# A two-layer decoder trunk: sinks loaded once, loads and stores on other queues, the combination in two parts, C's keys in two homes

## The chip, the cores and the metric

One core of a Trainium2 chip runs the whole program. The core has five engines that each work through a list of instructions of their own, in order: TensorE (PE in the rows; its weight loads PEld), VectorE (DVE), ScalarE (ACT), GpSimd (POOL) and SyncE (SP). A DMA is started by an instruction in the list of SyncE or of GpSimd, so it has a place in that list too: what stands behind a DMA that must wait for its buffer waits as well. The metric is the device time of one execution in microseconds (us), and a kernel's time is the median of its runs.

## The reference

The program computes two decoder layers on an input x of 512 rows by 1024 columns, in float32. One projection of x gives queries, keys, values and gates for three kinds of attention, A, B and C; their outputs are gated, projected and added, and a convolutional gated feed-forward part follows. The part that matters here, cut to its core:

```python
def hybrid_mixer(x, ...):
    proj = x @ w_in
    # A: 3 head groups (window, dilation), 8 heads each; the groups' outputs are
    #    weighted by a softmax over their log denominators
    for gi, (window, dil) in enumerate(A_GROUPS):
        o_g, lse_g = dilated_group_attention(...)
    wts = softmax(stack(lses), axis=0);  o_a = einsum('gbsh,gbshd->bshd', wts, stack(outs))
    # B: sliding window of 128, 8 heads, a learned sink logit per head in max and denominator
    m = maximum(logits.max(-1), sink);  p = exp(logits - m);  denom = p.sum(-1) + exp(sink - m)
    # C: latent attention, 8 heads, causal, 64 columns of key without and 32 with rotary position
    logits = (q_nope . k_nope + q_rope . k_rope) * scale
    merged = sum(sigmoid(gate_i) * (o_i @ w_branch[i]) for i in 3)
    return merged @ w_out
```

## The kernel before, in words

**Arithmetic.** float32 operands are split into a high part (ScalarE copies it) and a low part (VectorE subtracts), by `split_to` (L184, L185), and for weights at L76 and L77. A product is then three TensorE instructions, `mm3` (L178 to L180). Most are 128x128 weights against 512 columns; at the full clock such a one starts 0.227 us after the last.

**Stages of a layer.** The latents of C (`latp`), then A's projections with A's attention running between them, then B's projections, then a series of steps: gates (`gp`, 24 instructions each) and branch projections (`bp`, 12 each), in the order that the table `STEPS` gives, and then the output projection and the feed-forward part. The branch projections take A's output first, then B's, then C's. Attention runs in the gaps of the projections: `Attention.gap` adds time to a budget and `step` takes items from a queue. An item has three phases, a step apart: `scores` (scp, the exponentials), `turn` (normalisation and the transposes `ptp`) and `values` (`op`, the output). Its `cost` is what it takes from the budget. So where a gap falls, items of A, B and C stand between gate and branch instructions. A scheduler then fixes the order on each engine; the lists of instructions shown below are its result.

**Buffers.** 23 slots of the pool `sp` (4 KB in each of 128 partitions) are handed round between weights' successors, queries, keys, probabilities, loaded outputs (`od`) and their split forms (`oth`, `otl`), and rotary intermediates (`rq`, `rh`, `rl`). A new tile waits until the last use of the one whose slot it takes, and a DMA out of a slot counts as a use until it has landed.

**The places that the change touches.**

- *Sinks.* In each layer a tile `sink` of 128x2x8 is loaded on SyncE (L394, called at L424) and negated on VectorE (L425). There is one buffer, so layer 1's load waits until B of layer 0 has used the last sink.
- *Outputs through DRAM.* Each attention's output `ot` is stored by GpSimd into `o_dram` (L562 for B, L1001 for A, L810 for C). `load_oT` (L471) loads it as two tiles `od` on SyncE, before the branch projections. `split_oT` transposes A's (`otp`, L485) and splits all.
- *A's combination.* Rows of A's groups are stored by GpSimd to `arow` (L639); `Combine` loads them (`ct`, L973, on SyncE) in its `turn` and weighs them on VectorE (`cmx` at L988 and on) in its `values`, for two halves of the heads with four tiles each.
- *C.* `RopeC.run` rotates queries, splits them into `rh` and `rl`, stores these to `rope_q` with GpSimd (L892) and copies the keys' rotary half into `ckh` and `ckl` (L897). There is one such pair of key tiles. `PairC.run` loads the queries' rotary part (`cqh`, `cql`, L945, GpSimd) and writes the pair's keys into `ckh` and `ckl`, for each of four pairs of heads; four tiles of queries follow it (`ItemC`), tile t with t+1 key tiles. The values of tiles 0 and 1, and of 2 and 3, are one run of `op` (8 and 16 instructions), whose result takes two ScalarE copies (L808), two VectorE additions (L809) and two stores (L810).

## Time and profile before

| | us |
|---|---|
| median of 3 runs | 2081.39 |
| lowest, highest | 2080.52, 2083.09 |
| the profiled execution | 2081.52 |
| its span | 2079.8 |

The span is what the trace covers; 1.7 us of the profiled execution lie around it. [...] A row of a timeline gives the start in us from the span's start, the duration, the engine and line, the operation as out<-in, and in brackets how long the engine had been idle before it and what ended that. Where several equal instructions follow each other they share a row, with xN. Matmul rows overlap, since TensorE is pipelined: the time from start to start is what one costs.

### The profile page before, as it was taken

How to read it: one execution, taken by the hardware profiler on the slowest of the kernel's cores; microseconds unless marked ns; L12 is line 12 of the kernel's file. 1: busy time of each engine (PE TensorE's matmuls, PEld its weight loads, DVE VectorE, ACT ScalarE, POOL GpSimd, SP SyncE). 2: the span in 40 equal slices, each digit the busy share in tenths (PEclk: the TensorE clock that was granted, in tenths of full speed). 3: DMA queues.
4: the chain of work that ended last, by engine and by line, in shares of the span. 5: the costliest groups of instructions: out<-in, count | busy, mean ns of one | idle time of the engine just before them, and what ended most of it. 6: DMA issues, size and time to landing. Idle time of an engine off the chain costs nothing. (4 is left out here: it accounts for less than half of the span.)

```text
span 2079.8 us, 28299 instructions
## 1 busy us (share of the span) xinstructions
PE 2029.4 (98%) x10466; PEld 1717.3 (83%) x10466; DVE 1235.6 (59%) x2531; ACT 906.9 (44%) x1850; POOL 204.0 (10%) x354
## 2 busy tenths in 40 slices
PE   8999999989999999999999999999999999999997
PEld 7888888878878888888888888887888888888885
DVE  5545667757646664356465546686675566635645
ACT  4544465645432343244235444655564315423431
POOL 1111211201100100000020212112110010000001
PEclk9999999989999999999999999999999999999998
DMA  6633444435336233333433333444433443333331
GB/s 183 210 88 100 129 96 130 132 75 115 101 94 193 71 92 97 98 99 97 121 104 92 93 94 118 115 132 118 117 86 95 146 118 101 97 94 103 92 96 56
DMA packets 317447, 228.13 MB, mean 110 GB/s; under 512 B 46603, under 2 KB 289244, under 8 KB 316797
## 3 DMA queue, kind: packets, MB, share of 16 engines
q1 hardware_dynamic: 306972, 204.60, 34.6%
q0 software_dynamic: 10336, 21.72, 3.7%
q8 instruction: 83, 1.36, 0.3%
q14 instruction: 56, 0.45, 0.1%
HBM read 206.63 MB, written 24.88 MB: 111 GB/s over the span
## 5 line engine op out<-in xcount | busy, mean ns | idle before, releaser
L77 DVE TENSOR_TENSOR wlo<-wraw,whi 128x1024 fp32r<-128x1024 f32 (+2 forms) x316 | 380.0, 1204 | 371.9 <-ACT whi L76 368.0
L76 ACT ACTIVATE whi<-wraw 128x1024 fp32r<-128x1024 f32 (+2 forms) x316 | 328.7, 1043 | 373.9 <-PE dnp L179 120.0
L179 PE MATMUL up<-xl,whi 128*128 128x512 f32 (+1 forms) x768 | 285.3, 372 | 0.4
L178 PE MATMUL up<-xh,whi 128*128 128x512 f32 (+1 forms) x768 | 284.2, 372 | 0.7 <-ACT xh L350 0.5
L180 PE MATMUL up<-xh,wlo 128*128 128x512 f32 (+1 forms) x768 | 284.5, 371 | 0.0
L178 PE MATMUL qkp<-xh,whi 128*128 128x512 f32 x464 | 185.2, 399 | 0.0
L180 PE MATMUL qkp<-xh,wlo 128*128 128x512 f32 x464 | 184.1, 397 | 0.0
L179 PE MATMUL qkp<-xl,whi 128*128 128x512 f32 x464 | 183.6, 396 | 0.0
L179 PEld LDWEIGHTS up<-xl,whi 128*128 128x128 f32 x768 | 144.6, 188 | 26.0 <-DVE xl L355 1.2
L178 PEld LDWEIGHTS up<-xh,whi 128*128 128x128 f32 x768 | 144.0, 188 | 26.6 <-ACT xh L350 1.6
L180 PEld LDWEIGHTS up<-xh,wlo 128*128 128x128 f32 x768 | 144.5, 188 | 25.0
L178 PE MATMUL gp<-xh,whi 128*128 128x512 f32 x384 | 153.7, 400 | 0.0
L179 PE MATMUL gp<-xl,whi 128*128 128x512 f32 x384 | 153.2, 399 | 0.0
L180 PE MATMUL gp<-xh,wlo 128*128 128x512 f32 x384 | 152.6, 397 | 0.0
L528 ACT ACTIVATE sb<-sb,row 128x128 f32<-128x128 f32 (+1 forms) x192 | 80.7, 422 | 136.3 <-DVE row L525 128.8
L179 PE MATMUL dnp<-wlo,hT 128*128 128x512 f32 x352 | 136.9, 389 | 0.0
L180 PE MATMUL dnp<-whi,hT 128*128 128x512 f32 x352 | 136.8, 389 | 0.0
L178 PE MATMUL dnp<-whi,hT 128*128 128x512 f32 x352 | 135.6, 389 | 0.0
L525 DVE CUSTOM_DVE_ANT_0 sb<-scp,bias 128x128 f32<-128x128 f32 (+1 forms) x192 | 54.5, 322 | 105.9 <-DMA arow<-row 92.2
L180 PEld LDWEIGHTS qkp<-xh,wlo 128*128 128x128 f32 x464 | 87.4, 188 | 16.8 <-issue 0.4
L178 PEld LDWEIGHTS qkp<-xh,whi 128*128 128x128 f32 x464 | 87.4, 188 | 15.8 <-ACT vv L184 0.4
L179 PEld LDWEIGHTS qkp<-xl,whi 128*128 128x128 f32 x464 | 87.5, 189 | 15.4 <-issue 0.6
(331 smaller groups left out, 4249.0 us busy)
## 6 DMA issues: line engine op xcount, KB each, us to landing
wraw<-in_w_in_dram SPq DMA_DIRECT2D x124, 512.0 KB, 3.9
wraw<-in_w_ffn_up_dram SPq DMA_DIRECT2D x88, 512.0 KB, 4.0
wraw<-in_w_ffn_down_dram SPq DMA_DIRECT2D x40, 512.0 KB, 3.8
wraw<-in_w_branch_dram SPq DMA_DIRECT2D x16, 512.0 KB, 3.7
wraw<-in_w_out_dram SPq DMA_DIRECT2D x16, 512.0 KB
arow<-row POOLq DMA_DIRECT2D x96, 66.0 KB, 2.5
ct<-arow SPq DMA_DIRECT2D x16, 396.0 KB, 3.6
od<-o_dram SPq DMA_DIRECT2D x12, 512.0 KB, 4.8
```

The lines of the kernel that those rows point to most:

```text
L76: nc.scalar.activation(hi[:, :n], raw[:, :n], AF.Copy)
L77: nc.vector.tensor_tensor(lo[:, :n], raw[:, :n], hi[:, :n].bitcast(F32), ALU.subtract)
L178: nc.tensor.matmul(o, lh, rh, start=start, stop=False)
L179: nc.tensor.matmul(o, lh, rl, start=False, stop=False)
L180: nc.tensor.matmul(o, ll, rh, start=False, stop=stop)
L525: nc.vector.tensor_tensor_reduce(v[:, h, :], pp[h], j.bias(h, nk), -j.scale, j.floor(h), ALU.add, ALU.min, self.st[:, h:h + 1])
L528: nc.scalar.activation(v[:, h, :], v[:, h, :], AF.Exp, bias=self.st[:, h:h + 1], scale=-1.0, accum_out=self.st[:, 2 + h:3 + h])
```

## The change

Four edits, in one diff:

1. One tile `sinks` holds both layers' sinks. It is loaded (two DMAs) and negated (one instruction) in layer 0 after the latents; the loads and negations of each layer are gone.
2. The loads of `od` (12) and of `ct` (16) move from SyncE's list to GpSimd's; the 8 stores to `rope_q` move from GpSimd's to SyncE's.
3. `Combine` keeps the load (cost 0.1); a new class `Weigh` has the arithmetic (cost 0.5). They stand in the queue as load 0, load 1, weigh 0, load 2, weigh 1, load 3, weigh 2, weigh 3.
4. C has two pairs of key tiles, used in turn by the pairs of heads, so the copies of the rotary half are done twice (eight instead of four on GpSimd per layer). The last tile of pairs 0 to 2 moves behind the projection of the next pair.

```diff
+    sinks = cp.tile([P, DEPTH, 2, 8], F32, name="sinks")
...
-        sink = cp.tile([P, 2, 8], F32, name="sink", tag="sink")
-        bcast(I["sinks"], l * 8, 8, sink[:, 0])
-        nc.vector.tensor_scalar(sink[:, 1], sink[:, 0], -1.0, None, op0=ALU.mult)
+        sink = sinks[:, l]
...
+        if l == 0:
+            for i in range(DEPTH):
+                bcast(I["sinks"], i * 8, 8, sinks[:, i, 0])
+            nc.vector.tensor_scalar(sinks[:, :, 1], sinks[:, :, 0], -1.0, None, op0=ALU.mult)
...
-                nc.sync.dma_start(od[a], dap(o_dram[i], a * 2 * P * 512, [[512, P], [P * 512, 2], [1, 512]]))
+                nc.gpsimd.dma_start(od[a], dap(o_dram[i], a * 2 * P * 512, [[512, P], [P * 512, 2], [1, 512]]))
...
-                att.queue.extend(Combine(hf, t) for t in range(NT))
+                cs = [Combine(hf, t) for t in range(NT)]
+                att.queue.extend((*cs[:2], Weigh(cs[0]), cs[2], Weigh(cs[1]), cs[3], Weigh(cs[2]), Weigh(cs[3])))
...
-                return self.q[0][:, h, qs], self.q[1][:, h, qs], keys_c[0][:, h, ks], keys_c[1][:, h, ks]
+                return self.q[0][:, h, qs], self.q[1][:, h, qs], self.k[0][:, h, ks], self.k[1][:, h, ks]
...
-                        nc.gpsimd.dma_start(dap(rope_q, (i * 8 + x) * 32 * S, [[64 * S, 4], [S, 32], [1, S]]),
+                        nc.sync.dma_start(dap(rope_q, (i * 8 + x) * 32 * S, [[64 * S, 4], [S, 32], [1, S]]),
                                             hl[i][:, x].bitcast(F32))
-                keys_c.extend(slot(nm, F32R).rearrange("p (h n) -> p h n", h=2) for nm in ("ckh", "ckl"))
-                for h, b in enumerate((slice(64, P), slice(0, 64))):
-                    for i in range(2):
-                        nc.gpsimd.tensor_copy(keys_c[i][b, h, :], latT[3][b, i, :])
+                for c in range(2):
+                    keys_c.append([slot(nm, F32R).rearrange("p (h n) -> p h n", h=2) for nm in ("ckh", "ckl")])
+                    for h, b in enumerate((slice(64, P), slice(0, 64))):
+                        for i in range(2):
+                            nc.gpsimd.tensor_copy(keys_c[c][i][b, h, :], latT[3][b, i, :])
...
-                nc.sync.dma_start(self.ct, dap(arow[self.hf], self.t * P * 264, [[264, P], [S * 264, 3], [1, 264]]))
+                nc.gpsimd.dma_start(self.ct, dap(arow[self.hf], self.t * P * 264, [[264, P], [S * 264, 3], [1, 264]]))
...
+        late = [i for i in items_c if isinstance(i, ItemC) and i.t == NT - 1 and i.job.c < 3]
+        for item in late:
+            items_c.remove(item)
+            items_c.insert(1 + next(n for n, i in enumerate(items_c)
+                                    if isinstance(i, PairC) and i.job.c == item.job.c + 1), item)
```

TensorE's instructions are the same in number and kind; their order differs between A's first projections and the output projection of each layer.

**VectorE where A's output is transposed, layer 0, before.** The tile sb is B's probabilities, bst their statistics, otl the low part of A's transposed output.

```order
L751 TENSOR_SCALAR sb<-sb,bst 128x256 x2
L748 RECIPROCAL bst<-bst 128x2
L185 TENSOR_TENSOR otl<-otp,oth 128x2x128 x2
L425 TENSOR_SCALAR sink<-sink 128x8
L751 TENSOR_SCALAR sb<-sb,bst 128x256 x2
L185 TENSOR_TENSOR otl<-otp,oth 128x2x128 x5
```

**The same place after.** L756 and L753 are the lines L751 and L748 of before.

```order
L753 RECIPROCAL bst<-bst 128x2 x2
L756 TENSOR_SCALAR sb<-sb,bst 128x256 x3
L185 TENSOR_TENSOR otl<-otp,oth 128x2x128
L756 TENSOR_SCALAR sb<-sb,bst 128x256
L185 TENSOR_TENSOR otl<-otp,oth 128x2x128 x6
```

The negation of the next layer's sinks is gone from between the otl splits; the rest keeps its kind and nearly its order.

**SyncE from the branch weights of A to C's second chunk, layer 0, before.** These are loads of weights (wraw, craw), of A's output and of a table.

```order
L63 DMA wraw<-in_w_branch_dram 128x4x256 x4
L471 DMA od<-o_dram_435 128x2x512 x2
L63 DMA wraw<-in_w_in_dram 128x8x128
L877 DMA ropeT<-rope_T 128x2x512
L908 DMA craw<-in_w_ukv_dram 128x4x64
L63 DMA wraw<-in_w_in_dram 128x8x128 x2
L394 DMA sink<-in_sinks_dram 128x8
L63 DMA wraw<-in_w_branch_dram 64x4x256 x2
```

**The same place after.**

```order
L63 DMA wraw<-in_w_branch_dram 128x4x256 x4
L63 DMA wraw<-in_w_in_dram 128x8x128
L886 DMA ropeT<-rope_T 128x2x512
L918 DMA craw<-in_w_ukv_dram 128x4x64
L901 DMA rope_q<-rh 4x32x512 x2
L63 DMA wraw<-in_w_in_dram 128x8x128
L901 DMA rope_q<-rl 4x32x512 x2
L63 DMA wraw<-in_w_in_dram 128x8x128
L63 DMA wraw<-in_w_branch_dram 64x4x256 x2
```

The two od loads and the sink load have left this list, and the four stores of rotated queries stand in it, around a weight load.

**TensorE at the end of C in layer 1, before.** The rows are the last gate before C's last values (op) and the branch projection of B (bp) that goes on beside them; the eight ptp of the last tile stand 17 rows ahead of the first.

```order
L178 MATMUL gp<-xh,whi 128x512
L179 MATMUL gp<-xl,whi 128x512
L180 MATMUL gp<-xh,wlo 128x512
L804 MATMUL op<-ph,cv 128x256
L178 MATMUL gp<-xh,whi 128x512
L804 MATMUL op<-ph,cv 128x128
L179 MATMUL gp<-xl,whi 128x512
L180 MATMUL gp<-xh,wlo 128x512
L178 MATMUL bp<-oth,whi 128x512
L179 MATMUL bp<-otl,whi 128x512
L804 MATMUL op<-pl,cv 128x128
L804 MATMUL op<-ph,cv 128x256
```

**The same place after:** from the last gate row before the last transposes to the first values.

```order
L180 MATMUL gp<-xh,wlo 128x512
L794 MATMUL ptp<-ident,sb 128x128 x8
L809 MATMUL op<-ph,cv 128x256
L809 MATMUL op<-ph,cv 128x128
L809 MATMUL op<-pl,cv 128x128
L809 MATMUL op<-ph,cv 128x256
```

**And the end of those values, after, up to the first branch projection of C's output.**

```order
L809 MATMUL op<-pl,cv 128x256
L809 MATMUL op<-ph,cv 128x256
L809 MATMUL op<-pl,cv 128x256 x2
L178 MATMUL bp<-oth,whi 128x512
L178 MATMUL gp<-xh,whi 128x512
L179 MATMUL gp<-xl,whi 128x512
```

Before, 20 gate rows stood between the eight transposes and the first value, four more gate and branch rows between the first values, and the rest of B's branch and the whole last gates between the last value and the first bp of C. After, the transposes, the 16 values and that first bp stand in a row, and the gates' rows ahead of and behind them. Layer 0 has the same three pieces in a row after; before, it had 20 rows between transposes and values and 18 between the last value and that bp.

## Rows read from the trace of the kernel before

**Rows 1.** The page's first part: busy time, share and instructions of TensorE.

```profile
PE 2029.4 (98%) x10466; PEld 1717.3 (83%) x10466; DVE 1235.6 (59%) x2531; ACT 906.9 (44%) x1850; POOL 204.0 (10%) x354
```

**Rows 2.** Windows of 20 us: length, PE busy (count), granted clock, DMA share, GB/s.

```profile
400.00:420.00 20.00, 13.97 (x108) 0.89 0.54 126
420.00:440.00 20.00, 16.92 (x96) 0.77 0.18 45
480.00:500.00 20.00, 18.40 (x104) 1.00 0.26 62
1440.00:1460.00 20.00, 16.01 (x99) 0.74 0.37 81
1580.00:1600.00 20.00, 20.00 (x108) 1.00 0.37 111
```

**Rows 3.** The same view, the stretches at half clock.

```profile
353.00:356.40 3.40, 3.35 (x13) 0.67 0.36 84
415.50:429.20 13.70, 7.24 (x25) 0.50 0.18 49
586.00:593.00 7.00, 6.13 (x14) 0.52 0.43 144
1443.00:1453.30 10.30, 7.98 (x36) 0.50 0.43 106
```

**Rows 4.** Timeline of layer 0's transposes of A's output, TensorE: start, us, instruction, wait.

```profile
422.61 1.09 PE L485 MATMUL otp<-ident,od 128*128 128x128 f32 x4 [5.93 <-DVE otl L185]
```

**Rows 5.** The same stretch on VectorE.

```profile
421.44 0.17 DVE L425 TENSOR_SCALAR sink<-sink 128x8 f32<-128x8 f32 x1 [5.61 <-DMA sink<-in_sinks_dram]
```

**Rows 6.** ScalarE in the same place, layer 0.

```profile
413.06 0.38 ACT L184 ACTIVATE oth<-otp 128x256 fp32r<-128x256 f32 x1 [1.61 <-DMA rope_q<-rh]
```

**Rows 7.** ScalarE in the same place, layer 1.

```profile
1443.47 0.38 ACT L184 ACTIVATE oth<-otp 128x256 fp32r<-128x256 f32 x1 [3.02 <-DMA rope_q<-rh]
```

**Rows 8.** DMA issues: transfer, queue, count, KB, median us to landing.

```profile
od<-o_dram SPq DMA_DIRECT2D x12, 512.0 KB, 4.8
...
rope_q<-rh POOLq DMA_DIRECT2D x4, 256.0 KB, 7.9
rope_q<-rl POOLq DMA_DIRECT2D x4, 256.0 KB, 11.4
```

**Rows 9.** The tile rl: durations in ns, first and last start in us.

```profile
L892 POOL DMA_DIRECT2D rope_q<-rl x4: 691/692/700, 407.9 to 1437.8; - x4
L185 DVE TENSOR_TENSOR rl<-rq,rh x2: 1215/1217/1219, 404.2 to 1433.2; 128x1024 fp32r<-128x1024 f32 x2
```

**Rows 10.** From A to B in layer 0, TensorE's timeline.

```profile
353.05 0.33 PE L516 MATMUL scp<-ksh,q 128*128 128x128 f32 x1 [1.65 <-DVE bst L525]
```

**Rows 11.** The same stretch on VectorE.

```profile
350.53 0.17 DVE L988 TENSOR_REDUCE cmx<-ct 128x4 f32<-128x12 f32 x1 [3.07 <-DMA ct<-arow]
```

**Rows 12.** C's scores in layer 0, TensorE's timeline.

```profile
487.80 0.50 PE L523 MATMUL scp<-ckh,cqh 128*128 128x512 f32 x1 [1.40 <-DVE bst L525]
```

**Rows 13.** The end of C in layer 0, TensorE's timeline.

```profile
571.52 1.03 PE L789 MATMUL ptp<-ident,sb 128*128 128x128 f32 x8
...
579.98 0.40 PE L178 MATMUL gp<-xh,whi 128*128 128x512 f32 x1
...
586.87 0.80 PE L178 MATMUL bp<-oth,whi 128*128 128x512 f32 x1 [2.63 <-ACT oth L184]
```

**Rows 14.** The same stretch on VectorE.

```profile
572.79 1.29 DVE L185 TENSOR_TENSOR pl<-ptp,ph 128x512 fp32r<-128x512 f32 x2 [3.51 <-ACT ph L184]
```

**Rows 15.** The same stretch on ScalarE.

```profile
581.05 0.38 ACT L808 ACTIVATE ot<-op 64x256 f32<-64x256 f32 x1 [0.48 <-DVE ot L809]
...
585.77 1.05 ACT L184 ACTIVATE oth<-od 128x1024 fp32r<-128x1024 f32 x1
```

**Rows 16.** The same stretch on SyncE's queue.

```profile
584.34 0.37 SPq L471 DMA_DIRECT2D od<-o_dram  x1
```

**Rows 17.** GpSimd's first copy of the rotary keys, layer 0.

```profile
405.43 0.61 POOL L897 CAST ckh<-latT 64x512 fp32r<-64x512 f32 x1
```

More of the change, by code (lines that the diff above doesn't have):

```diff
@@ L817, in __init__, with k @@
                 self.c, self.vh = c, 2 * (c % 2)
+            @property
+            def k(self):
+                return keys_c[self.c % 2]
             def normalize(self, item, n):
@@ L956, in run @@
                 for h in range(2):
-                    split_to(*(a[HALF[h], h, :] for a in keys_c), p[HALF[h]])
+                    split_to(*(a[HALF[h], h, :] for a in j.k), p[HALF[h]])
         arow = [dp.tile([3, S, 264], F32, name=f"arow{h}", tag=f"arow{h}") for h in range(2)]
         class Combine:
-            cost, mixer = 0.6, 0
+            cost, mixer = 0.1, 0
             def __init__(self, hf, t):
@@ L972, in turn, with __init__, scores, values @@
                 self.ct = sp.tile([P, 3, 264], F32, name="ct", tag="s")
-                nc.sync.dma_start(self.ct, dap(arow[self.hf], self.t * P * 264, [[264, P], [S * 264, 3], [1, 264]]))
+                nc.gpsimd.dma_start(self.ct, dap(arow[self.hf], self.t * P * 264, [[264, P], [S * 264, 3], [1, 264]]))
             def values(self):
-                ct = self.ct.rearrange("p g (r n) -> p g r n", r=2)
+                pass
+        class Weigh:
+            cost, mixer = 0.5, 0
+            def __init__(self, c):
+                self.c, self.hf, self.t = c, c.hf, c.t
+            def scores(self):
+                pass
+            def turn(self):
+                pass
+            def values(self):
+                ct = self.c.ct.rearrange("p g (r n) -> p g r n", r=2)
                 nm, lv = (ct[:, :, :, c:c + 2].rearrange("p g r h -> p (g r) h") for c in (P, P + 2))
```

## The prediction

> **What bounds the kernel now.** I read the page's first part first: TensorE is busy for 2029.4 of 2079.8 us [rows 1], and the change leaves its instructions as they are. So all that can be won or lost is TensorE's waiting and the stretches in which it runs at half clock. The windows come next, since these losses sit in a few places. Where A's output is transposed in layer 0, 400 to 440 has 13.97 and 16.92 of 20 us busy [rows 2], 9.1 idle; the 7.24 us of work in the stretch at clock 0.50 [rows 3] would have taken half of that, so 3.6 more are lost, 12.7 in all. The same place in layer 1 has 4.0 idle [rows 2] and 7.98 busy at 0.50 [rows 3], so 4.0 + 4.0 = 8.0. From A to B in layer 0 there is one wait of 1.65 [rows 10] with 3.4 us at 0.67 behind it [rows 3], some 1.7 more. In C's scores of layer 0 a wait of 1.40 [rows 12] stands alone, with the clock at 1.00 around it [rows 2]. At the end of C in layer 0 there is a wait of 2.63 [rows 13], then 7.0 us at 0.52 [rows 3], so about 3.4 more, 6.0 in all; the end of C in layer 1 loses nothing (20.00 of 20.00 busy at 1.00 [rows 2]). The timelines of VectorE, ScalarE and SyncE say what ended each of these waits.
>
> **Sinks.** In layer 0 VectorE stood 5.61 us before the negation, until the sinks of layer 1 had landed [rows 5], with the splits of A's transposed output behind it, and TensorE waited 5.93 for these [rows 4]. After the change no such instruction stands there. Layer 1 has the same place without a sink load, so I take what it shows as what is left: 12.7 - 8.0 = **-4.7 us**. Bounds: -12.7, if all losses of that place hang on it, and 0, if the next wait (below) ends as late. The new negation and two small loads stand at the start among the latents, where ScalarE's weight split waits for a weight load anyway; I cost them at nothing, and if that cover is gone it is one short landing, inside the range.
>
> **Stores of rotated queries on SyncE.** Before, ScalarE's first oth waited for the store of rh, 1.61 us in layer 0 [rows 6] and 3.02 in layer 1 [rows 7], because it takes that tile's slot; TensorE's waits of layer 1 hang on this. After, the list of ScalarE has the first oth without a DMA to wait for, and the second oth behind both stores of rl. So one wait goes and another comes. The low part rl is ready at 404.2 + 1.2 = 405.4 in layer 0 and 1434.4 in layer 1 [rows 9]; with one weight load ahead of it SyncE can issue at once. Landing takes 11.4 us on GpSimd's queue [rows 8]: 416.8 and 1445.8. The second oth of before came 1.2 us after the first, at 414.3 and 1444.7. So it is later by 2.5 and 1.1: **+3.6 us**. Behind the waiting instruction stand ScalarE's other oth, the copies of B's results and C's first weights, and TensorE waits for these. Bounds: -4.6 (both waits of rows 6 and 7 gone, nothing in their place), and +9.5, if the rl stores land when they did before, 11.4 us after GpSimd's issues at 407.9 and 1437.8 [rows 9], that is at 419.3 and 1449.2. The weight loads behind these stores on SyncE wait only for their issue; I cost that at nothing, covered by the loads that are always some chunks ahead.
>
> A 256 KB store takes 7.9 and 11.4 us while a 512 KB load takes 4.8 [rows 8]: these stores are slow for their size. [...]
>
> **A's combination.** VectorE stood 3.07 us before a `cmx` for a `ct` [rows 11], whose load SyncE could issue only once rows of A had been stored; TensorE then waited 1.65 and lost 1.7 more to the clock. On GpSimd each ct stands right behind the store that it needs, and the arithmetic one item later, so this wait may go (-3.35). But each ct now also holds up the row stores behind it until the one before has landed, and the first `cmx` stands earlier in VectorE's list than it did, so a wait of the same kind can come there (0, or 2 us worse). Neither row is nearer; I take the middle, **-1.7 us**.
>
> **C's keys in two homes.** The wait of 1.40 before the fourth tile's scores may go, since that tile now comes a projection later: **-1.4 us**, bounds 0 and -1.4. Four more copies per layer on GpSimd, 0.61 each [rows 17], are wanted only when the second pair is projected; I cost them at nothing, and 2.4 us in each layer if a load of queries behind them comes too late.
>
> **The end of C.** Here the reordering costs, in both layers. After, eight ptp, the 16 values and the first bp of C's output stand in a row, with no gate rows between. In the trace the eight ptp are through at 571.52 + 1.03 = 572.55 [rows 13], and the low parts that the values need at 572.79 + 1.29 = 574.08 [rows 14]: 1.5 us without work. After the last value TensorE is free at 579.98 [rows 13]; the second `ot` copy ends at 581.05 + 0.38 = 581.43, and the split oth behind it takes 1.05 [rows 15]: 582.5, so 2.5 us without work. Before, 18 gate rows stood there in layer 0 and 34 rows in layer 1. The second tile of od is loaded once the last store has landed, 584.34 [rows 16], 4.4 after the last value, plus 4.8 [rows 8] and 1.05, so 10.2; TensorE wants it 26 instructions of 0.227 after that first bp, at 8.4 (later at half clock): 0 to 1.8, taken as 0. A single wait of 2.63 brought about 7 us at half clock [rows 3, 13]; two waits of 1.5 and 2.5 within some 4 us are nearest to that row, 3.4 more. So 1.5 + 2.5 + 3.4 = 7.4 in each layer, against 6.0 in layer 0 and 0 in layer 1: 14.8 - 6.0 = **+8.8 us**. Bounds: +2.0 (no clock loss) and +14.
>
> **The sum** against the profiled execution's 2081.52 (1.7 of it outside the span; the median is 2081.39, so no correction): -4.7 + 3.6 - 1.7 - 1.4 + 8.8 = +4.6, so **2086.1 us**. The other od loads (A's and B's) change queue with gate work beside them, and I cost them at nothing.
>
> **Rivals.**
>
> *The stores land early on SyncE* (not slower). If rl is home by 414, no oth waits, and of the 8.0 that the place loses in each layer the wait of 3.0 [rows 7] and the 4.0 of clock [rows 3] go too: 2086.1 - 3.6 - 2 x 7.0 = 2068.5. For it: SyncE issues them earlier and GpSimd's copies no longer stand between. Against it: the size of the landing times in rows 8. It decides at 414.3 and 1444.7. Chance 0.17.
>
> *The end of C stays at full clock* or its waits are covered in part: 2086.1 - 6.8 = 2079.3. For it: the wait of 1.40 that left the clock alone; against it: the 2.63 that did not. Chance 0.16.
>
> *The four stores are bound by what they move, not by when they are issued:* rl lands as late as before, +9.5 in place of +3.6, so 2092.0. For it: the second two took 11.4 us and the first two 7.9, as if they had stood behind them. [...]
>
> *The loads on GpSimd don't do what they are moved for:* a ct or od waits for the same stores wherever it is issued; then the -1.7 is 0 and the time 2087.8, inside the forecast's own range, 2083 to 2090.
>
> **How the numbers follow.** The forecast has 0.40, the first three rivals 0.55 together, and 0.05 is left for what I don't see. About 0.2% is what a measurement of this kernel can tell from no change, 4.2 us. Faster by more: the first rival and a little of the rest, 0.20. Within: the second rival and the part of the forecast below 2085.6, 0.32. Slower: the rest, 0.48. The range leaves out the first rival and little of the third: 2075 to 2094.
>
> **What would show it right or wrong.** In the profile after: no wait of VectorE for sinks; ScalarE's second oth in A's transposes waiting for a store of rl; at the end of C in both layers a wait of about 1.5 before op and 2.5 before the first bp, with half clock behind. It is wrong if the time of these three places together is under 20 us, or if a wait appears in C's scores or before A's first branch that no term here names.

## The result and the profile after

| | us |
|---|---|
| before, median of 3 runs | 2081.39 |
| after, median of 3 runs | 2117.95 (2116.03 to 2118.73) |
| ratio after / before, 95% interval | 1.0174 (1.0158 to 1.0190) |
| the profiled execution of after, its span | 2118.73, 2117.0 |

The change costs 36.6 us. TensorE has the same 10466 instructions but is busy for 2045.3 us instead of 2029.4 [rows 1] in a span that is 37.2 longer, so it idles 21.3 us more. Its mean granted clock over the span is 0.985 in place of before's 0.989: of the span, 31.8 us are lost to half clock in place of 22.9, so at most 9 of the 15.9 us of added busy time are half clock. The rest of it is not told apart. The page's first part:

```profile
PE 2045.3 (97%) x10466; PEld 1726.0 (82%) x10466; DVE 1238.1 (58%) x2530; ACT 906.7 (43%) x1850; POOL 228.8 (11%) x382
```

The start times of the same TensorE instructions in the two traces give a ledger by stage (layer 0, layer 1): the start -1.4; A's projections +9.1, +7.5; from there to A's transposes +0.2, +3.8; the transposes -0.3, +4.7; the stage from the first branch projection to the output projection, with C in it, +5.0, +13.0; feed-forward 0; behind the last matmul -4.4. The last one belongs to the queue moves (see the queues below).

Windows of 20 us of after, columns as in [rows 2]:

```profile
200.00:220.00 20.00, 16.85 (x73) 0.91 0.49 144
420.00:440.00 20.00, 12.96 (x72) 0.74 0.29 84
520.00:540.00 20.00, 17.43 (x71) 0.83 0.35 89
580.00:600.00 20.00, 16.27 (x88) 1.00 0.43 119
600.00:620.00 20.00, 19.53 (x78) 0.91 0.30 86
1460.00:1480.00 20.00, 11.74 (x77) 0.64 0.36 111
1570.00:1590.00 20.00, 17.30 (x78) 0.91 0.29 80
1640.00:1660.00 20.00, 16.62 (x68) 0.83 0.22 61
```

What the clock takes in such a window is 20 us times what it lacks of 1.00: 1.8 us at 0.91, 3.4 at 0.83.

Four kinds of place lose. The first is new: A's projections, where the prediction has no term. VectorE, then TensorE, then GpSimd, layer 0:

```profile
215.94 0.17 DVE L1014 TENSOR_REDUCE cmx<-ct 128x4 f32<-128x12 f32 x1 [6.00 <-DMA ct<-arow]
...
267.57 0.29 DVE L529 CUSTOM_DVE_ANT_0 sb<-scp,bias 128x128 f32<-128x128 f32 x1 [3.82 <-DMA arow<-row]
```

```profile
208.68 0.50 PE L178 MATMUL vp<-xh,whi 128*128 128x512 f32 x1 [2.12 <-DVE q L188]
...
223.17 0.36 PE L178 MATMUL scp<-kh,q 128*128 128x256 f32 x1 [1.65 <-DVE cw__2109 L1020]
```

```profile
212.12 1.56 POOL L983 DMA_DIRECT2D ct<-arow  x2 [3.62 <-DMA arow<-row]
```

VectorE stands 6.0 us before the first weighing, from 209.94 on, until its `ct` has landed; splits of keys that TensorE wants are queued behind it, and TensorE's wait of 1.65 comes behind the weighing. TensorE's wait of 2.12 is another one: it ended at 208.68, before VectorE began to stand. There TensorE wants the split of the queries at once, because the six `scp` rows that stood between the last `op` and the first `vp` in before are now further down its list. Later VectorE stands 3.8 us before it takes new scores, until an older row's store has landed (a row buffer comes free). Such waits of VectorE are in before too (23.9 us in 13 of them from 185 to 300, against 19.4 in 10 here); TensorE's waits for these scores are 1.2 us there and 2.5 here.

The second is the place of [rows 4 to 7]. ScalarE in layer 0, then SyncE, then TensorE there:

```profile
421.03 0.69 ACT L1077 ACTIVATE mg<-gp,bg 128x512 f32<-128x512 f32 x1 [6.07 <-DMA rope_q<-rh]
...
428.25 0.66 ACT L184 ACTIVATE oth<-otp 128x256 fp32r<-128x256 f32 x2 [1.49 <-DMA rope_q<-rl]
```

```profile
411.54 1.20 SPq L901 DMA_DIRECT2D rope_q<-rh  x2
...
413.90 4.64 SPq L901 DMA_DIRECT2D rope_q<-rl  x2
```

```profile
424.80 0.37 PE L178 MATMUL op<-pT,bv 128*64 128x128 f32 x1 [6.56 <-ACT ot L565]
```

VectorE's wait for sinks [rows 5] is gone. In its place ScalarE waits 6.07 (in layer 1 6.63) for rh's store, not at the first `oth` [rows 6, 7] but earlier in its list, at the first tile of gates `mg`, with the copy `ot` of B's results behind it that TensorE waits for. The wait for rl at the second `oth` comes on top. SyncE issues the two stores of rl 3.7 us apart (413.90 and 417.59). The four issues of rl in both layers, durations in ns (lowest, median, highest); in before none took over 700 [rows 9]:

```profile
L901 SPq DMA_DIRECT2D rope_q<-rl x4: 945/2122/3640, 413.9 to 1462.7; - x4
```

The third is C's projections and scores, where the last tile of a pair now stands behind the next pair's projection. TensorE in layer 0 (layer 1 has 0.78, 0.78, 0.83 and 0.87):

```profile
503.66 0.50 PE L178 MATMUL gp<-xh,whi 128*128 128x512 f32 x1 [0.78 <-DVE gs L1097]
...
527.91 0.50 PE L178 MATMUL cp<-latT,cwh 128*128 128x512 f32 x1 [0.78 <-ACT gs L1077]
...
529.70 0.33 PE L527 MATMUL scp<-ckh,cqh 128*128 128x128 f32 x1 [0.82 <-DVE bst L529]
...
531.98 0.79 PE L178 MATMUL bp<-oth,whi 128*128 128x512 f32 x1 [0.75 <-DVE cql L185]
```

With the clock behind them (3.4 us in 520 to 540, 1.8 in 1570 to 1590) that is 6.5 and 5.1 us, where before had 1.4 [rows 12] and nothing.

The fourth is the end of C, TensorE in layer 0 (layer 1 has 1.29, 0.51 and 2.28 in the same rows):

```profile
594.94 0.81 PE L809 MATMUL op<-ph,cv 128*128 128x256 f32 x2 [1.29 <-ACT ph L184]
596.27 0.33 PE L809 MATMUL op<-pl,cv 128*128 128x128 f32 x1 [0.51 <-DVE pl L185]
...
600.46 0.50 PE L178 MATMUL bp<-oth,whi 128*128 128x512 f32 x1 [2.28 <-ACT oth L184]
```

With 1.8 us of clock behind it in 600 to 620 and 3.4 in 1640 to 1660 it is 5.9 and 7.5 us; before lost 6.0 and nothing. So of the +5.0 and +13.0, about 5 us in each layer are C's projections.

### The profile page after: what moved, and what is told of

It is laid out like the page before. It is cut to its first block, busy times and chain, and to the rows that moved or that the text cites. A ratio compares the mean times of both kernels' runs of the same rounds, so it can differ in the third digit from the quotient of the medians.

```text
span 2117.0 us, 28288 instructions
## 1 busy us (share of the span) xinstructions
PE 2045.3 (97%) x10466; PEld 1726.0 (82%) x10466; DVE 1238.1 (58%) x2530; ACT 906.7 (43%) x1850; POOL 228.8 (11%) x382
## 5 line engine op out<-in xcount | busy, mean ns | idle before, releaser
L643 POOL DMA_DIRECT2D arow<-row x96 | 52.1, 543 | 456.0 <-DVE row L640 148.1
```

Source lines behind the costliest of these rows:

```text
L643: nc.gpsimd.dma_start(dap(arow[self.hf], (self.g * S + first) * 264 + self.c * 132, [[step * 264, P], [1, 132]]), item.row)
```

## The experiments

A kernel's effect is read from its ratio to before on the same chip. "Over sinks_only" is (ratio - 0.9968) x 2077. The intervals are 0.0009 to 0.0017 of the ratio to either side, so differences under 3 to 4 us say nothing. Executions of one kernel spread over 2 to 8 us (those of before on one chip over 3 to 12), and a trace is one of them: a stage's number from one trace can be off by 1 to 3 us.

| kernel | median us | ratio (interval) | over sinks_only |
|---|---|---|---|
| sinks_only | 2069.66 | 0.9968 (0.9957 to 0.9979) | 0 |
| sinks_comb | 2093.79 | 1.0086 (1.0069 to 1.0103) | +24 |
| sinks_queues | 2072.70 | 0.9982 (0.9971 to 0.9992) | +3 |
| sinks_keys | 2085.08 | 1.0042 (1.0027 to 1.0057) | +15 |
| comb_no_wait | 2073.45 | 0.9981 (0.9971 to 0.9990) | +3 |
| comb_pairs | 2090.44 | 1.0060 (1.0045 to 1.0075) | +19 |
| comb_late | 2085.13 | 1.0040 (1.0026 to 1.0054) | +15 |
| comb_rows | 2080.01 | 1.0011 (1.0002 to 1.0020) | +9 |
| homes_slots | 2079.85 | 1.0009 (0.9999 to 1.0018) | +8.5 |
| slots_shift | 2071.33 | 0.9975 (0.9966 to 0.9984) | +1.5 |
| homes_later | 2074.71 | 0.9985 (0.9975 to 0.9994) | +3.5 |
| od_gpsimd | 2071.28 | 0.9964 (0.9953 to 0.9976) | -1 |
| rope_sync | 2066.56 | 0.9947 (0.9931 to 0.9963) | -4 |
| ct_gpsimd | 2066.67 | 0.9943 (0.9928 to 0.9958) | -5 |
| rope_od | 2072.12 | 0.9978 (0.9967 to 0.9989) | +2 |
| comb_whole | 2099.03 | 1.0103 (1.0087 to 1.0118) | after -15 |
| after_rows | 2105.88 | 1.0133 (1.0116 to 1.0150) | after -8.5 |
| ct_rows | 2060.15 | 0.9913 (0.9898 to 0.9927) | -11 |

### One part at a time: sinks_only, sinks_comb, sinks_queues, sinks_keys

Before with the sinks edit alone, and then with one other part of the diff each, word for word as it stands there:

```diff
+    sinks = cp.tile([P, DEPTH, 2, 8], F32, name="sinks")
...
+                cs = [Combine(hf, t) for t in range(NT)]
...
-                        nc.gpsimd.dma_start(dap(rope_q, (i * 8 + x) * 32 * S, [[64 * S, 4], [S, 32], [1, S]]),
+                        nc.sync.dma_start(dap(rope_q, (i * 8 + x) * 32 * S, [[64 * S, 4], [S, 32], [1, S]]),
...
+        late = [i for i in items_c if isinstance(i, ItemC) and i.t == NT - 1 and i.job.c < 3]
```

> Before with the sinks edit alone. Theory: the wait of 5.6 us on VectorE in layer 0 goes and layer 0's transposes of A's output then lose what layer 1's do, so 4 to 6 us faster, 2075 to 2077. Rival: the store of rotated queries that ScalarE waits for there ends as late, the gain is swallowed, 2080 to 2082.

> The sinks edit and the parted combination, its loads still on SyncE. Theory (the 9.1 and 7.5 us that A's projections lost in the changed kernel come from its loads standing in GpSimd's list): within 2 us of the sinks edit alone. Rival (they come from the parting, which puts VectorE's first reduction earlier and pulls items forward): 8 to 17 us slower than the sinks edit alone.

> The sinks edit and all three queue moves, combination and C as before. Theory (queues carry the losses of A's projections, and of A's transposes through the stores of rotated queries on SyncE): 20 to 28 us slower than the sinks edit alone, with 7 to 9 in each layer's projections of A and 3 to 6 in each layer's transposes. Rival (the parting carries the first): 6 to 12 us slower, all in the transposes.

> The sinks edit, the two homes of C's keys and the late tiles; queues and combination as before. Theory (the order at the end of C leaves 1.5 and 2.5 us without work and half clock behind, and the projections have waits of their own): 8 to 16 us slower than the sinks edit alone, all from the first branch projection on. Rival (that order comes from the queues' timing and not from the late tiles): within 3 us.

The sinks gain 7 us. The parting costs 24, more than either side expected, the queues 3, less than either, the keys 15. The theory that the queues carry A's loss falls. The three sum to 42, and after stands 43 over sinks_only, but that is luck: inside the change the parting is worth 15 (comb_whole below), and the queues and the keys together 28 in place of 18. In sinks_comb VectorE's rows show both waits of after, with the loads of ct still on SyncE, and TensorE has the second one too:

```profile
215.20 0.17 DVE L1009 TENSOR_REDUCE cmx<-ct 128x4 f32<-128x12 f32 x1 [6.23 <-DMA ct<-arow]
...
268.00 0.29 DVE L529 CUSTOM_DVE_ANT_0 sb<-scp,bias 128x128 f32<-128x128 f32 x1 [4.82 <-DMA arow<-row]
```

```profile
268.66 0.55 PE L178 MATMUL scp<-kh,q 128*128 128x256 f32 x1 [2.89 <-DVE row L529]
```

Against sinks_only its TensorE is 7.0 us later after the first place and 5.0 more after the second; in layer 1 it is 7.7 and 2.2.

### What the parting costs: comb_no_wait, comb_pairs, comb_late, comb_rows

comb_no_wait reads another DRAM tensor in the first half, so that half weighs other numbers with the same instructions:

```diff
-                nc.sync.dma_start(self.ct, dap(arow[self.hf], self.t * P * 264, [[264, P], [S * 264, 3], [1, 264]]))
+                nc.sync.dma_start(self.ct, dap(arow[1], self.t * P * 264, [[264, P], [S * 264, 3], [1, 264]]) if self.hf else
+                                  dap(I["w_branch"], self.t * P * 264, [[264, P], [S * 264, 3], [1, 264]]))
```

> sinks_comb (the sinks edit and the parted combination), but the loads of the first half's ct read a weight in DRAM of the same size instead of the stored rows of A, so nothing has to be stored before them; A's combination of the first half therefore weighs wrong numbers, with the same instructions. Theory: in sinks_comb VectorE reaches the first cmx 17 instructions earlier than before and stands 6.2 us there until its ct has landed, and the split keys and queries behind it come late; this wait is what A's projections of layer 0 and 1 lose (+12.4, +9.7). Then no such wait is in this trace, and at least 8 us of each layer come back: about 2073 to 2078. Rival: the loss is the place of the arithmetic in the list (VectorE's work of a combination stands ahead of the splits that TensorE wants next, whenever its load lands); then it stays within 5 us of sinks_comb, 2089 to 2094.

```profile
204.22 0.23 DVE L1010 TENSOR_REDUCE cmx<-ct 128x4 f32<-128x12 f32 x2
...
258.86 0.29 DVE L529 CUSTOM_DVE_ANT_0 sb<-scp,bias 128x128 f32<-128x128 f32 x1 [3.88 <-DMA arow<-row]
```

VectorE's rows: the first weighing runs at 204.22 without a wait, and nearly all the cost goes. The scheduler, which has no store to wait for here, also orders the lists anew: some 300 of TensorE's 1576 instructions in layer 0's projections of A stand in another order, the split of the queries comes earlier, and TensorE's wait of 2.1 for it, which sinks_comb has as well, is gone too. So this run takes away the wait for ct and that order together. The second wait stays.

comb_pairs puts each weighing right behind its load:

```diff
-                att.queue.extend((*cs[:2], Weigh(cs[0]), cs[2], Weigh(cs[1]), cs[3], Weigh(cs[2]), Weigh(cs[3])))
+                att.queue.extend(x for c in cs for x in (c, Weigh(c)))
```

> The sinks edit and the combination in two classes, but each load is followed at once by its own weighing in the queue, with the same two costs (0.1, then 0.5) that the parting gives. Theory of the wait: with only one step between the load and its weighing VectorE meets the ct earlier still, so it waits at least as long for every ct, and the time is that of sinks_comb or worse, 2092 to 2105. Rival, the staggering of the queue (load, load, weigh, load, weigh ...) is what costs: then it falls back to within 5 us of sinks_only, 2069 to 2075.

The wait is there again (5.31 us, at 215.40), and so are 19 us: the staggered queue isn't the cause. The time is a little under the 2092 expected at least.

```diff
+                if j == 3 and c == 0:
+                    att.queue.extend(weighs)
...
-                att.queue.extend((*cs[:2], Weigh(cs[0]), cs[2], Weigh(cs[1]), cs[3], Weigh(cs[2]), Weigh(cs[3])))
+                att.queue.extend(cs)
+                if hf:
+                    att.queue.extend(Weigh(c) for c in cs)
+                else:
+                    weighs.extend(Weigh(c) for c in cs)
```

> The sinks edit and the combination in two parts, but of the first half of the heads the four weighings stand in the queue behind the first four tiles of the next job (its loads stay where they were), and of the second half behind the four loads. VectorE's first cmx then stands at the place in its list that it has with the whole combination, 18 instructions later than in sinks_comb. Theory: what sinks_comb lost (about 10 us in each layer among A's projections) was that VectorE met ct before it had landed; then no wait of over 2 us for ct is left in the first half, and the time is 2069 to 2077. Rival: parting the item costs by itself (more steps, more slots held by ct, a changed order on TensorE); then it stays above 2083.

VectorE's rows:

```profile
216.36 0.17 DVE L1017 TENSOR_REDUCE cmx<-ct 128x4 f32<-128x12 f32 x1 [0.98 <-DMA ct<-arow]
...
260.12 0.29 DVE L529 CUSTOM_DVE_ANT_0 sb<-scp,bias 128x128 f32<-128x128 f32 x1 [4.51 <-DMA arow<-row]
```

A miss. The wait for ct is under 1 us and the 7 us of the first place are gone, as the theory had it, but 15 us remain: in layer 0 TensorE loses 4.7 at the second place, and 3.6 between A and B, where the second half's order is a new one too (it waits 2.15 and 2.41 there, sinks_only once 1.84). So the wait for ct is not all of it.

```diff
-                item.row = tp.tile([P, 132], F32, name="row", tag="row", bufs=4)
+                item.row = tp.tile([P, 132], F32, name="row", tag="row", bufs=6)
```

> sinks_comb (the sinks edit and the parted combination) with six buffers instead of four for A's rows (row, 128x132), so that VectorE needn't wait for the store of the row four tiles back before it takes the next scores. Theory: of the 24 us that the parting costs, some 10 (6.8 in layer 0 and 2.5 in layer 1 in the stretch of the first job after the combination) are this wait, which the parted items meet because they let the items behind them start earlier; then VectorE's waits for row stores of 3 to 5 us are gone there and the time falls by 6 to 12, to 2082 to 2088 by the chip of sinks_comb. Rival: the row buffers are not what holds, TensorE waits as long for something else, and the time stays within 4 us of sinks_comb.

Windows 240 to 280 of sinks_comb, then of comb_rows:

```profile
240.00:260.00 20.00, 19.74 (x115) 1.00 0.37 106
260.00:280.00 20.00, 17.11 (x116) 0.83 0.23 69
```

```profile
240.00:260.00 20.00, 20.00 (x126) 1.00 0.38 105
260.00:280.00 20.00, 20.00 (x137) 1.00 0.34 88
```

Six row buffers give back 15.6 of the 24, more than expected; the first wait (6.02 for ct) is still in that trace. The starts of the same projections of A, against sinks_only, tell the two places apart. The table has what TensorE loses at the first place (up to 30 us behind the first weighing) and from there to the end of A's projections, in us, for layer 0 and layer 1; each is a median over the projections of a stretch:

| kernel | first place | second place |
|---|---|---|
| sinks_comb | 7.0, 7.7 | 5.0, 2.2 |
| comb_no_wait | -1.5, -1.2 | 3.3, 2.8 |
| comb_pairs | 7.1, 5.8 | 1.8, 4.0 |
| comb_late | 0.2, 0.3 | 4.7, 3.9 |
| comb_rows | 6.5, 6.6 | -1.2, -0.3 |
| after | 7.4, 7.3 | 1.6, 2.1 |
| after_rows | 6.4, 7.8 | -1.2, -0.1 |
| comb_whole | 0.0, 0.3 | 0.7, 1.6 |

The first place costs 6 to 8 us in each layer wherever VectorE waits 5 to 6 us for ct, with four row buffers or six, and nothing where that wait is gone. The second costs the parted kernels 2 to 5 us with four row buffers and nothing with six. So the parting is dear in two places with two causes. Within the first, the wait for ct and the order of the lists around it are not told apart: in after, TensorE's wait of 2.12 and the 1.8 us of half clock behind it, about half of the 7.4, come before VectorE's wait can reach it.

TensorE's gap of 2.89 us at the second place is gone with two buffers more, and of VectorE's waits for the store of an older row (ten of them, 21.3 us, from 185 to 300 in sinks_comb) one of 1.8 is left in comb_rows.

### What the two homes cost: homes_slots, slots_shift, homes_later

homes_slots is sinks_keys without the `late` lines.

> The sinks edit and C's two pairs of key tiles, with all of C's items in the order of before (no tile moved behind the next pair's projection). sinks_keys cost 15.4 us over sinks_only: +4.4 and +2.9 before A's transposes in the two layers, +2.3 and +7.9 at the end of C. Theory: the first part is the two tiles more that are taken from the ring of slots (a tile of gates then takes the slot of rh, and ScalarE waits 4 to 5 us there for the store), the second is the moved tiles; then this kernel has that wait of ScalarE again, loses 7 to 8 us before A's transposes, nothing at the end of C, and stands at +6 to +9 over sinks_only, near 2077. Rival: the moved tiles carry all of it, by the order of the whole list; then it stands within 2 us of sinks_only, near 2070.

It stands where the theory put it, 8.5 over sinks_only, though it loses 9 at the end of C in layer 1, where the theory had nothing (see below). The other 7 us of sinks_keys come with the moved tiles. The two traces have 6.1 of them in layer 0, where TensorE waits 3.02 us in C's scores (1.34 in homes_slots) with half clock behind it; in layer 1 that wait is 2.98 against 2.20, and nothing more is lost. sinks_keys, layer 0:

```profile
513.76 0.45 PE L527 MATMUL scp<-ckh,cqh 128*128 128x128 f32 x1 [3.02 <-DVE cql L185]
```

```diff
                         nc.gpsimd.tensor_copy(keys_c[i][b, h, :], latT[3][b, i, :])
+                for _ in range(2):
+                    nc.gpsimd.memset(slot("idle")[:1, :1], 0.0)
```

> The sinks edit, one pair of key tiles as before, and behind the copies into it two tiles more taken from the ring of slots, in which GpSimd writes one zero each and which nobody reads. homes_slots cost 8.5 us over sinks_only with C's items in the order of before. Theory: it is only that the ring is two places further, so that the first tile of gates takes rh's slot and ScalarE waits there for its store; then this kernel, which holds no second keys and copies nothing, has the same wait of 4 to 5 us and stands 6 to 10 over sinks_only, 2078 to 2082. Rival: the eight copies on GpSimd (0.61 to 0.75 us each), which stand between the stores of rh and rl, are the cost; then it stands within 3 us of sinks_only, 2069 to 2074.

ScalarE in slots_shift, layer 0, and TensorE:

```profile
411.79 1.26 ACT L1052 ACTIVATE mg<-gp,bg 128x512 f32<-128x512 f32 x2 [5.12 <-DMA rope_q<-rh]
```

```profile
414.35 0.37 PE L178 MATMUL op<-pT,bv 128*64 128x128 f32 x1 [6.21 <-ACT ot L565]
```

Two slots that nobody uses bring the wait of `mg`, without a second home and without its copies: that mechanism is the theory's. Its time is not, and lies where the rival, the copies, had it: the trace loses 3.8 and 5.4 us against sinks_only in the transposes of the two layers, yet the median is only 1.5 higher. Layer 0 gets 2.0 of it back up to the output projection, layer 1 nothing, and the traced execution (2074.2) was at the upper end of the ten. How much the wait is worth by itself stays open between 1.5 and 9. What homes_slots has beyond it in the traces is at the end of C in layer 1 (8.8 us against 0.1), and no row there waits for a copy.

```diff
+            def home(self, c):
+                keys_c[c] = [slot(nm, F32R).rearrange("p (h n) -> p h n", h=2) for nm in ("ckh", "ckl")]
...
+                if j.c == 1:
+                    chunks_c[0].home(1)
```

> homes_slots with the second pair of key tiles taken from the ring (and its rotary halves copied) only when the second pair of heads is projected, after the gates' tiles have been taken. Theory: two homes cost by the place where they shift the ring; then the first tile of gates has no store to wait for, A's transposes lose nothing against sinks_only (homes_slots: 4.1 and 4.3 us), and the time is 2069 to 2075. Rival: what homes_slots lost is the order of C's last items, which changes with any two slots more; then the end of C in layer 1 still loses 7 to 9 us and the time is 2076 to 2081.

ScalarE and TensorE in homes_later:

```profile
410.21 0.38 ACT L184 ACTIVATE oth<-otp 128x256 fp32r<-128x256 f32 x1 [1.58 <-DMA rope_q<-rh]
```

```profile
1599.38 0.50 PE L178 MATMUL bp<-oth,whi 128*128 128x512 f32 x1 [2.63 <-ACT oth L184]
```

With the same homes taken later, `mg` waits for nothing and the store is met at the `oth` again; 5 of the 8.5 us go. Both theories have a part: the end of C in layer 1 still loses some 7 us in this trace, by a wait of 2.63. In homes_slots it loses 9 with no tile moved at all, by the wait that after has:

```profile
1602.19 0.50 PE L178 MATMUL bp<-oth,whi 128*128 128x512 f32 x1 [2.28 <-ACT oth L184]
```

### The queues: od_gpsimd, rope_sync, ct_gpsimd, rope_od

Each is sinks_only with the named lines' engine changed as in the diff.

> The sinks edit and the loads of od on GpSimd's queue, nothing else moved. sinks_queues, which also has ct and the stores of rotated queries on other queues, cost 3.0 us over sinks_only: A's transposes +2 in each layer, the end of C in layer 1 +7, and less elsewhere. Theory: the end of C in layer 1 is od's (a row of values and the first branch instruction that now stand side by side, with ScalarE's split of od behind the second load), and A's transposes are the rotated queries' stores; then this kernel loses 4 to 7 us at the end of C in layer 1 and nothing before A's transposes: 2073 to 2077. Rival: the end of C in layer 1 moves by the order that the stores bring, and od costs nothing: within 1.5 us of sinks_only.

> The sinks edit and the stores of rotated queries on SyncE's queue, nothing else. The prediction put them at +3.6 over the two layers: the wait for rh's store goes from ScalarE's first oth, and one for the stores of rl comes at its second, later by 2.5 and 1.1 us. sinks_queues, with three moves, cost 3.0. By that step this kernel stands 2 to 6 us over sinks_only, 2072 to 2076 by the chip of sinks_only. Rival: the store of rh lands as late from either queue, the wait stays where it was, and the time is within 1.5 us of sinks_only.

> The sinks edit and the loads of ct on GpSimd's queue, nothing else. sinks_queues cost 3.0 us, of which the stores of rotated queries alone gave back 4.4 and od alone 0.8. If the three add up, the loads of ct cost 6 to 10 us: 2076 to 2080 by the chip of sinks_only. They stand in GpSimd's list ahead of the clearing of kh and kl for the next job and of later row stores. Rival: the three don't add up (the order of the last items of C is what sinks_queues lost), and the loads of ct alone stay within 2 us of sinks_only.

> The sinks edit, the stores of rotated queries on SyncE and the loads of od on GpSimd: the change without its two dear parts (the parting and the two homes) and without ct. If the effects add up, -4.4 and -0.8 on sinks_only: ratio 0.993 to 0.996 of before, some 10 to 13 us under it. Rival: od behind the other moves delays the end of C in layer 1, as in sinks_queues (+7 in its trace): ratio 0.997 to 0.999.

Alone, two of the three moves gain 4 and 5 us, just clear of the noise and against both sides of what was expected, and od is level; together they cost 3, and rope_od costs 2, as its rival had it, where -5 would be the sum. Three readings are clear. ScalarE in sinks_only, then rope_sync:

```profile
413.15 0.38 ACT L184 ACTIVATE oth<-otp 128x256 fp32r<-128x256 f32 x1 [1.47 <-DMA rope_q<-rh]
```

```profile
411.27 0.38 ACT L184 ACTIVATE oth<-otp 128x256 fp32r<-128x256 f32 x1 [2.04 <-DMA rope_q<-rh]
```

The first `oth` still waits for rh's store, issued from 401.30 on by SyncE against 403.98 by GpSimd; its wait ends about as long after that issue (9.97 and 9.17 us), so it ends 2 us earlier. And ct: VectorE between A and B in layer 0, sinks_only, then ct_gpsimd:

```profile
350.98 0.17 DVE L992 TENSOR_REDUCE cmx<-ct 128x4 f32<-128x12 f32 x1 [3.54 <-DMA ct<-arow]
```

```profile
356.19 0.17 DVE L992 TENSOR_REDUCE cmx<-ct 128x4 f32<-128x12 f32 x1 [0.28 <-DMA ct<-arow]
```

The wait of [rows 11] goes, and TensorE's of [rows 10] with it; another wait of VectorE for ct stands earlier, 3.81 us at 342.53, and TensorE has 0.7 behind these in place of sinks_only's 1.84.

But that isn't where ct_gpsimd's 5 us are. Up to its last matmul its trace is 0.5 us behind that of sinks_only; 4.6 us are won after it. The program ends with a DRAIN, an instruction of GpSimd's list that begins 3.6 us after the last matmul in every trace; the program's last line, durations in ns (lowest, median, highest), in sinks_only, ct_gpsimd, od_gpsimd, rope_sync, rope_od and after:

```profile
L1261 POOLq DRAIN  x3: 40/93/9854, 2056.5 to 2066.8; - x3
L1261 POOLq DRAIN  x3: 40/93/4787, 2057.0 to 2062.7; - x3
L1261 POOLq DRAIN  x3: 40/102/3152, 2066.8 to 2073.1; - x3
L1261 POOLq DRAIN  x3: 40/102/8379, 2057.5 to 2066.4; - x3
L1261 POOLq DRAIN  x3: 40/93/9769, 2058.1 to 2068.4; - x3
L1288 POOLq DRAIN  x3: 40/102/4626, 2110.7 to 2116.7; - x3
```

It takes 9.85 us in all eleven traces in which GpSimd issues 222 transfers, 4.63 in the four with 242 (after among them) and 4.79 in the two with 238 (ct_gpsimd, ct_rows). The time behind the last matmul is 14.2, 9.8 and 9.6 us there. So the moves change the program's end, and not by adding up: against sinks_only that end is 1.5 shorter in rope_sync, 4.1 in od_gpsimd and 4.6 in ct_gpsimd, but 4.4 with all three and 0.1 in rope_od. That is about 6 of the 13 us by which the three together miss their sum, and 5.5 of the 7 of rope_od. Why the length follows the number of transfers, and not in step with it, no run shows.

The rest sits at the end of C. All traces with od on GpSimd (od_gpsimd, sinks_queues, rope_od) lose 5 to 7 us in the stage that holds the end of C in layer 1, by a wait before C's first branch product; rope_sync and ct_gpsimd have none. But od_gpsimd's median shows it only net of the shorter end, and its traced execution was the slowest of its seven. TensorE in od_gpsimd:

```profile
1602.94 0.79 PE L178 MATMUL bp<-oth,whi 128*128 128x512 f32 x1 [2.63 <-ACT oth L184]
```

### The changed kernel itself, and a better one: comb_whole, after_rows, ct_rows

comb_whole is after with the old `Combine`; after_rows is after with six row buffers; ct_rows is sinks_only with the loads of ct on GpSimd and six row buffers.

> The changed kernel with the combination in one piece again (loads of ct stay on GpSimd), all other edits kept. Theory: the parting is a cost of its own, as sinks_comb showed without the other edits (24.1 us over sinks_only), so 20 to 26 us come back: 2091 to 2098. Rival: with ct on GpSimd's queue, where each load stands behind the store that it needs, the wait is another one and the parting is worth less than 10 us there; then it stays above 2107.

> The changed kernel with six buffers instead of four for A's rows, nothing else. comb_whole, with the combination in one piece, stood 14.8 us under the changed kernel; in sinks_comb six buffers gave back 15.6 of 24.1. Theory: the row buffers are the larger part of what the parting costs here too, so 6 to 14 us come back: 2099 to 2107 (ratio 1.0095 to 1.0135). Rival: in the changed kernel it is the wait for ct itself (6.0 us of VectorE) and the other edits; then under 4 us come back: ratio above 1.015.

> The sinks edit, the loads of ct on GpSimd, and six row buffers, the combination in one piece. ct_gpsimd stood at 0.9943 of before. Theory: in ct_gpsimd TensorE still waits 1.4 and 0.9 us among A's projections of the second half for scores that VectorE takes after a row's store; with six buffers these go, and 2 to 5 us come: ratio 0.992 to 0.9935. Rival: with the combination whole the row buffers hold nobody on the path, and the changed order of the lists decides: 0.994 to 0.997.

In after the parting is worth 15 us, not 24: neither side had that. Without it 28 us over sinks_only are left, where sinks_queues and sinks_keys cost 18 apart. The traces show where the two meet: in A's transposes, which lose 15.9 us in comb_whole's two layers against 7.2 in sinks_keys and 4.0 in sinks_queues. The slots bring the wait of `mg` for rh, and the stores on SyncE bring one for rl behind it, which neither kernel has alone. ScalarE in comb_whole, layer 0 (6.13 and 3.40 in layer 1):

```profile
410.61 0.69 ACT L1060 ACTIVATE mg<-gp,bg 128x512 f32<-128x512 f32 x1 [5.60 <-DMA rope_q<-rh]
...
417.44 0.38 ACT L184 ACTIVATE oth<-otp 128x256 fp32r<-128x256 f32 x1 [3.11 <-DMA rope_q<-rl]
```

TensorE waits 5.65 and then 2.69 us for the copies `ot` behind these; sinks_keys has 6.01 there and no second wait.

Six row buffers alone give back 8.5 of after, as expected. ct_rows beats both kernels: 2060.15 us, 18 under before and 54 under after by the ratios (0.9913 and 1.0174), a little more than expected. Of its 11 us under sinks_only, 4.6 are the shorter end. The page's first part:

```profile
PE 2020.1 (98%) x10466; PEld 1714.6 (83%) x10466; DVE 1236.7 (60%) x2530; ACT 912.5 (44%) x1850; POOL 217.1 (11%) x370
```

## Why the prediction was wrong

It forecast 2086.1 in 2075 to 2094, slower by 4.7; the kernel is slower by 36.6. The sign came out right, but most of the time lies where the sum had little or nothing: A's projections, at 0, lost 16.6; the place of sinks, rotated queries and ct, at -2.8, lost 8.4; C's keys, at -1.4, lost 10; the end of C, at +8.8, lost 7 to 8; the start and the program's end, at 0, gained 5.8. By its steps:

- **Sinks, -4.7: right.** sinks_only gained 7 us, and its trace has 5.9 at the place named. No wait for sinks is left.
- **A's combination, -1.7: the step that failed.** Its ct half holds for TensorE: ct on GpSimd takes the wait of [rows 10] away; in after 0.36 of it is left, with 1.06 at a gate row ahead. VectorE still waits 3.47 and 1.95 us for ct there in after, and what ct_gpsimd gained came from the program's end. Its parting half had "0, or 2 us worse" for the earlier `cmx`. Measured: 24 us alone, 15 inside the change. The bound was taken from the waits of the second half [rows 11]. The first half was not looked at, because it had little to gain (VectorE waited 1.1 us there, TensorE not for it); but a ct can't land before the last rows of its half have been stored: the first `cmx` ran 6 to 7 us after GpSimd issued the last of these stores, whole or parted (213.60 to 219.47 in sinks_only, 208.31 to 215.20 in sinks_comb), while the parted weighing stands 18 instructions earlier in VectorE's list (16 in after). And no term asked what the parting does to the order of the lists around it, or to the tiles behind: these ran into the four row buffers. No term prices A's projections, in effect a price of 0, with 16.6 us behind it in the trace of after.
- **Rope stores on SyncE, +3.6: right places, cause half right.** That one wait goes from the first `oth` and another comes at the second is in the rows of after. But the first had only moved to `mg`, further up the list, and grown to 6.07 and 6.63: I looked at the `oth` rows of ScalarE's list and not at whoever else now takes rh's slot. And it is the second pair of key tiles that moved it (slots_shift), not the queue, which alone gained 4 us, 1.5 of them at the program's end. The wait for rl came only where both edits meet (comb_whole). It ended 14.4 us after rl was ready and SyncE began to issue its stores (413.90 to 428.25), not 11.4 as priced: SyncE began the second of them only at 417.59, 3.7 us after the first, where GpSimd took 0.7 in before [rows 9]. From its own issue that store took 10.7. So the price of a landing was right and the two issues at once were not; the end is as late as the third rival (chance 0.22) had it. Its reason, stores bound by what they move, is not shown, and no run tells why SyncE began the second store 3.7 us after the first.
- **Two homes, -1.4: wrong sign.** No row waits for the copies, as assumed, though no run has them without the slots. The two slots were not counted at all, and in a ring of 23 that many kinds of tile share they shift who waits for whom. Measured +8.5 with the slots, +15 with the moved tiles. The wait of 1.40 in C's scores [rows 12] did go, but four waits of 0.8 and half clock came among C's projections in both layers, 10 us in the trace of after: the sign that the prediction's last paragraph named, a wait in C's scores.
- **The end of C, +8.8: sizes right, cause half right.** 1.5 and 2.5 were expected without work, 1.8 and 2.28 came, in both layers; the clock took 1.8 us in layer 0 (0.91 in 600 to 620, behind the wait) and 3.4 in layer 1 (0.83 in 1640 to 1660), where 3.4 had been taken for each; and the second od load costs TensorE nothing, as taken. But in layer 1 homes_slots shows the same without a moved tile: the rows between the last value and the first branch product are filled by whatever the list's order happens to leave, and several edits of the change empty them.
- **The range** left out what the sum left out. The last paragraph of the prediction named one sign of that error ("a wait that no term here names", in C's scores); it should have had a chance and a price. For A's projections it had no sign at all.

## What to carry to other kernels

Price the place where a change has nothing to win, too: an instruction that comes earlier in an engine's list meets its load earlier, and the load comes no sooner behind the stores that it needs: the first weighing ran 6.9 us after the last of these was issued in sinks_comb and 5.9 in sinks_only, with a wait of 6.2 us in place of 1.1. When a tile is added to a shared ring, list who takes the slots of the tiles with slow stores (here `rh`, for whose stores ScalarE waited 6.1 and 6.6 us), before and after, for every engine. When work is spread so that the next items start earlier, check the number of buffers of what those items produce: here six row buffers in place of four gave 8.5 and 16 us where the combination was parted, and 6 (ct_gpsimd to ct_rows) where it was whole.

## What was not expected of the hardware

GpSimd's DRAIN at the program's end is not the same for every program: 3.15 to 9.85 us, the same to 0.01 us wherever GpSimd issues the same number of transfers (222 or 242), and where it takes 8.4 us or more the span ends 0.8 us behind it (13.46 and 14.24 us behind the last matmul in sinks_only, 11.98 and 12.76 in rope_sync); with the shorter ones the span ends 9.6 to 10.2 us behind the last matmul. A pair of 256 KB stores of rotated queries took 9 to 10 us from the first issue to the wait's end from either queue; of the pair behind it, the second issue began 3.7 us after the first on SyncE in after and 0.7 on GpSimd in before. And small moves between queues (rope, ct, od: -4, -5, -1 apart, +3 together) don't add up, in part by that DRAIN and in part because a scheduler rebuilds the lists: for these, only the whole kernel's time counts, not a stage of one trace.
